# Two-mixer decoder layer: weight sums by adding DMAs, and x sums begun at the attention's end

## The chip, the cores and the metric

The kernel runs on one core of a Trainium2 chip. The metric is device microseconds of one execution, from outside the program; a profiled execution also gives the span from its first instruction to its last. A core has TensorE (PE, matmuls; its weight loads show as PEld), VectorE (DVE), ScalarE (ACT), GpSimd (POOL) and SyncE (SP), each with a queue of its own that is worked off in order, and 16 DMA engines.

## The reference, cut to what matters

One layer with two attention mixers, A (8 heads) and B (8 heads in 2 groups), on 512 tokens of width 1024, all float32:

```python
h = rms_norm(x, norm_w)
proj = h @ w_in                      # q, k, v, z of both mixers, ..., gate_m (2 * 1024 columns)
o_a = moba_mixer(...)                # block-sparse attention
o_b = nsa_mixer(...)                 # compressed, selected and window attention
y_a = o_a * silu(z_a);  y_b = o_b * silu(z_b)
g_m = sigmoid(gate_m)
merged = g_m[..., :1024] * (y_a @ w_branch_a) + g_m[..., 1024:] * (y_b @ w_branch_b)
x = x + merged @ w_out
```

The change concerns two of the products: the second half of `gate_m` (the gates of mixer B, `h` times a 1024x1024 part of `w_in`) and `merged @ w_out`.

## The kernel before, in words

Every large product is made with three fp32r matmuls (`mm3`, line 416): an operand is split in a high part `hi` and a rest `lo`, and hi·hi, hi·lo and lo·hi are summed in PSUM. A weight tile `wr` (128x512, 256 KB) is loaded by SP, ACT or POOL casts it to `wh` (lines 337 and 339), and DVE or POOL subtracts to get `wl` (line 341). The class `Stream` holds the list of all weight tiles in the order of their use, with 6 raw buffers and 8 pairs of `wh` and `wl`; a raw buffer becomes free for the next load when its `wl` is made.

The order of each engine's queue is fixed when the program is built. A planner in the kernel runs three generators (attention, projections and products, compression) against a clock `now`, in ns. A `Chain` is a row of steps; each step goes to the engine that the planner's costs say is done first, at the planner's time. So the planner's costs and times settle which engine does a step and where it stands. The hardware then waits for data, not for the planner's clock.

The stages, by the profile: the first projections, then the attention with projections as filler between its steps until about 338 us; the last gates of mixer A (`gmgate`); eight branch products of mixer A (`pbr`, 341 to 363 us), during which DVE also makes sums of x; the gates of mixer B (`gate_pair`, `pgw`) with the branch products of mixer B, to 425 us; and the output product (`last_wino`, `po`).

The steps of the attention that the prediction speaks of: for each unit (a head and a branch) DVE makes `sb` and row statistics, ACT makes `P` (exp), DVE the reciprocal `sst`, POOL multiplies `P` (line 992, four blocks of 512, 384, 256 and 128 columns; a small `p` where two units share a block), PE transposes it (`pt`, line 1001), ACT and DVE split the result in `ph` and `pl` (a last part is copied to `pf`), and PE multiplies with v into `O`.

The products with 1024x1024 weights are made by Winograd's form of Strassen's scheme: the weights are four quadrants a11, a12, a21, a22 and seven half-size products replace eight. It needs four sums of weight quadrants and four sums on the other side. Before, `Group` in the `Stream` makes the weight sums on the core: `ws` (line 378) from raw tiles in SBUF, by DVE or POOL, and `ws` is split like a raw tile. The x sums for mixer B's gates (`x_again`) start when both the attention and mixer A's gates are done: x is loaded again (`xa`), ACT scales it (line 1291), DVE and POOL make `ta` and `tb` (lines 1301 to 1305), and both are split into hi and lo (lines 1308 to 1313). `m_sums` does the same for the output product.

Lines that matter in the tail: 1392 (`gm` times `pbr`, which frees one of the two PSUM buffers of `pbr`), 1445 to 1449 (merge and split), 1481 to 1488 (`m_sums`) and 1519 (`xr`, the sum of a product into the output rows).

Of the kernel before, what the change touches and what calls it, by code (L numbers as in the profile page):

```python
# [18 lines left out]
S = 512  # L19
# [20 lines left out]
WGATES = True  # L40
WOUT = True
# [48 lines left out]
def hybrid_kernel(ctx: ExitStack, tc: tile.TileContext, x, x0, xT, wtok, wchan, gains, w1,  # L90
# [193 lines left out]
    class Group:  # L284


        def __init__(g, raws, outs):
            g.raws, g.outs = raws, outs
            g.uses = {}
            for o in outs:  # L290
                for z in (o,) if isinstance(o, int) else o[1:3]:
                    g.uses[z] = g.uses.get(z, 0) + 1

    class Stream:


        def __init__(w, entries, bufs, hi, lo):
            w.bufs, w.mk_hi, w.mk_lo = bufs, hi, lo
            w.raws, w.outs = [], []
            for e in entries:  # L300
                r0, o0 = len(w.raws), len(w.outs)
                if isinstance(e, Group):
                    w.raws += e.raws
                    w.outs += [(e, k, r0, o0) for k in range(len(e.outs))]
                else:
                    w.raws.append(e)
                    w.outs.append((None, 0, r0, o0))
            w.raw, w.out, w.chain, w.i, w.loaded, w.freed = {}, {}, {}, 0, 0, 0
            w.left, w.sums = {}, {}
# [9 lines left out]
        def used(w, r, when=None):  # L319
            if r in w.sums:  # L320
                w.sums[r][2] -= 1
                if not w.sums[r][2]:
                    release(w.sums[r][0], when)
                return
            w.left[r] -= 1
            if not w.left[r]:
                w.freed += 1
                while w.loaded < len(w.raws) and w.loaded - w.freed < w.bufs:
                    w.load()

        def halves(w, c, i, n, raw, src):
            hi, lo = w.mk_hi()[:, :n], w.mk_lo()[:, :n]
            w.out[i] = hi, lo

            def f(e):
                if e is nc.scalar:
                    e.copy(hi, raw())  # L337
                else:
                    e.tensor_scalar(hi, raw(), 1.0, 1.0, op0=ALU.mult, op1=ALU.mult)
            c.do({"A": ca(n), "P": 78 + n}, f).mark((w, 0, i))  # L340
            c.do(either(n), lambda e: e.tensor_sub(lo, raw(), hi.bitcast(F32))).mark((w, 1, i))  # L341
            c.call(lambda: w.used(src, c.t))

        def split(w, upto):
            while len(w.chain) < min(upto, len(w.outs)):
                i = len(w.chain)
                g, k, r0, o0 = w.outs[i]
                o = 0 if g is None else g.outs[k]
                n = w.raws[r0][1]
                rs = [r0 + z for z in ((o,) if isinstance(o, int) else o[1:3]) if isinstance(z, int)]  # L350
                while w.loaded <= max(rs, default=-1):
# [11 lines left out]
                st = w.sums[key] = [None, [], g.uses.get(me, 0) + 1, None]
                c = w.chain[i] = Chain(held=True)
                ready = [max(now[0], *(w.raw[r][1] for r in rs))]
                wait = [w.sums[o0, z] for z in (xa, xb) if not isinstance(z, int)]
                get = lambda z, r0=r0, o0=o0: (w.raw[r0 + z][0] if isinstance(z, int) else w.sums[o0, z][0])
                idx = lambda z, r0=r0, o0=o0: r0 + z if isinstance(z, int) else (o0, z)

                def go(c=c, ready=ready, wait=wait):  # L370
                    if all(z[3] is not None for z in wait):
                        c.start(max(now[0], *ready, *(z[3] for z in wait)))

                def f(e, st=st, op=op, a=get(xa) if isinstance(xa, int) else xa, b=get(xb) if isinstance(xb, int) else xb,
                      get=get, tag=tag, n=n):
                    a, b = (z if not isinstance(z, str) else get(z) for z in (a, b))
                    st[0] = alloc(tag, "ws")
                    (e.tensor_add if op == "+" else e.tensor_sub)(st[0][:, :n], a, b)  # L378

                def after(c=c, st=st, xa=xa, xb=xb, idx=idx):  # L380
                    st[3] = c.t
                    for z in (xa, xb):
                        w.used(idx(z), c.t)
                    for fn in st[1]:
                        fn()
                c.do(either(n), f, None, tag).call(after)
                w.halves(c, i, n, lambda st=st, n=n: st[0][:, :n], key)
                pend = [z for z in wait if z[3] is None]
                for z in pend:
                    z[1].append(go)  # L390
                if not pend:
                    go()
# [176 lines left out]
    for j in range(8):  # L569
        tiles += chan_tiles(f"gm{j}")  # L570
    tiles += [(wbr[j, 0], 512) for j in range(8)]
    for j in range(4):
        if WGATES:
            (a11, a12), (a21, a22) = (chan_tiles(f"gm{8 + j + i}") for i in (0, 4))
            tiles.append(Group([a11, a12, a21, a22, (wbr[j, 1], 512)], [
                0, 1, ("+", 2, 3, "s1", "sb"), ("-", "s1", 0, "s2", "sb"), ("-", 1, "s2", "s4", "sb"),
                ("-", 0, 2, "s3", "sb"), 4, 3]))
            tiles.append((wbr[j + 4, 1], 512))
        else:
            for i in (0, 4):  # L580
# [679 lines left out]

    gms = {}

    def gmgate(w, j):
        t = att("gm", F32)

        def emit(ps):
# [418 lines left out]
```

## Time and profile before

| | us |
|---|---|
| median of 3 runs (475.29 to 476.2) | 475.5 |
| the profiled execution, its own time | 475.35 |
| its span | 473.4 |

The time outside the span is 1.95 us. Busy times within the span:

| engine | busy us (share) | instructions |
|---|---|---|
| PE | 463.6 (98%) | 3172 |
| PEld | 424.5 (90%) | 3172 |
| DVE | 399.2 (84%) | 994 |
| ACT | 288.8 (61%) | 693 |
| POOL | 171.8 (36%) | 218 |

Matmuls overlap each other, so a time lost on PE is read from the starts of neighbouring matmuls, not from the busy share. In the rows below, the first column is the start in us from the span's start, the second how long the row lasted (of a row that merges several instructions, all together), and the bracket at the end tells how long the engine sat idle before it and who ended the wait. The granted TensorE clock was 1.00 throughout.

### The profile page before, as it was taken

To read this page: it belongs to the slowest core of one execution; us is meant where nothing else is said; L and a number is where in the kernel's file an instruction comes from. 1 tells how busy PE (TensorE), PEld (TensorE's weight loads), DVE (VectorE), ACT (ScalarE), POOL (GpSimd) and SP (SyncE) were. 2 spreads that over 40 slices of the span, in tenths; PEclk is the share of its full clock that TensorE was granted. 3 is DMA by queue.
4 is the path that set the end of the run, shared out by engine and by line. 5 is a ranking of instruction groups with operands and counts; after the bars stand their busy time and mean duration, and the time that the engine had idled before them with its cause. 6 is when DMAs were issued, how large, how long until landed. Compare 5 with 4: busy or idle time off the path is not lost.

```text
span 473.4 us, 9154 instructions
## 1 busy us (share of the span) xinstructions
PE 463.6 (98%) x3172; PEld 424.5 (90%) x3172; DVE 399.2 (84%) x994; ACT 288.8 (61%) x693; POOL 171.8 (36%) x218
## 2 busy tenths in 40 slices
PE   9999999999999999999999999999999999999897
PEld 9999898999999989888888888888887999999897
DVE  6888899798898579888787877778599799989994
ACT  8576694486876347576587457677483466444431
POOL 1254373048666105344446025464234023141000
PEclk9999999999999999999999999999999999999999
DMA  8916234444344423122212322201730442277551
GB/s 305 280 55 188 77 79 136 138 115 129 92 115 123 126 67 91 46 66 69 71 42 66 75 74 75 66 32 39 242 113 24 135 133 70 65 243 238 172 172 68
DMA packets 30206, 53.41 MB, mean 113 GB/s; under 512 B 3344, under 2 KB 5776, under 8 KB 30160
## 3 DMA queue, kind: packets, MB, share of 16 engines
q1 hardware_dynamic: 30160, 52.83, 37.1%
q8 instruction: 25, 0.41, 0.4%
q14 instruction: 21, 0.17, 0.1%
HBM read 50.06 MB, written 2.75 MB: 112 GB/s over the span
## 4 chain that ended last, share of the span: by engine, by line
PE 80%; DVE 13%; ACT 2%; issue 2%; POOL 2%; POOLq 0%; DVEq 0%
PE pgc L416 19%; PE pgt L416 18%; PE pgw L416 8%; PE O L1035 6%; PE pbr L416 6%; PE pt L1001 5%; DVE wl L341 4%; PE po L416 3%; PE sps L954 3%; PE sps L955 3%; PE pgf L631 3%; DVE ws L378 1%; DVE xr L1519 1%; PE pq L886 1%; PE pw L475 1%
## 5 line engine op out<-in xcount | busy, mean ns | idle before, releaser
L416 PE MATMUL pgt<-wh,hh 128*128 128x256 f32 (+1 forms) x288 | 82.9, 288 | 1.6 <-DVE X L772 0.9
L416 PE MATMUL pgt<-wl,hh 128*128 128x256 f32 (+1 forms) x288 | 81.4, 283 | 0.2 <-DVE wl L341 0.2
L416 PE MATMUL pgt<-wh,hl 128*128 128x256 f32 (+1 forms) x288 | 81.2, 282 | 0.0
L341 DVE TENSOR_TENSOR wl<-wr,wh 128x512 fp32r<-128x512 f32 (+1 forms) x108 | 75.3, 703 | 4.4 <-ACT wh L337 3.9
L992 POOL TENSOR_SCALAR P<-P,sst,gate 128x512 f32<-128x512 f32 (+3 forms) x56 | 39.6, 712 | 63.8 <-DVE sst L991 49.7
L973 DVE CUSTOM_DVE_ANT_0 sb<-sps,T 128x512 f32<-128x512 f32 (+3 forms) x96 | 46.1, 485 | 18.8 <-PE sps L955 17.8
L416 PE MATMUL pgc<-hh,wh 128*128 128x512 f32 x144 | 59.4, 413 | 0.0
L416 PE MATMUL pgc<-hl,wh 128*128 128x512 f32 x144 | 56.8, 395 | 0.0
L416 PE MATMUL pgc<-hh,wl 128*128 128x512 f32 x144 | 56.8, 395 | 0.0
L988 ACT ACTIVATE P<-sb,sst 128x512 f32<-128x512 f32 (+3 forms) x88 | 50.8, 578 | 9.6 <-DVE sst L973 9.0
L416 PEld LDWEIGHTS pgt<-wh,hh 128*128 128x128 f32 x288 | 54.2, 188 | 2.6 <-PE pgt L416 1.0
L416 PEld LDWEIGHTS pgt<-wh,hl 128*128 128x128 f32 x288 | 54.2, 188 | 0.5
L416 PEld LDWEIGHTS pgt<-wl,hh 128*128 128x128 f32 x288 | 54.2, 188 | 0.4 <-DVE wl L341 0.4
L1013 ACT CAST ph<-pt 128x512 fp32r<-128x512 f32 (+2 forms) x72 | 33.2, 479 | 34.9 <-PE pt L1001 34.1
L337 ACT CAST wh<-wr 128x512 fp32r<-128x512 f32 (+1 forms) x81 | 49.4, 616 | 0.4 <-DMA wr<-in_wtok 0.2
L992 POOL TENSOR_SCALAR P<-P,sst 128x512 f32<-128x512 f32 (+3 forms) x32 | 24.9, 782 | 44.3 <-DVE sst L991 37.8
L1001 PE MATMUL pt<-cst,P 128*128 128x128 f32 x232 | 40.7, 272 | 0.2 <-POOL P L992 0.2
L1015 DVE TENSOR_TENSOR pl<-pt,ph 128x512 fp32r<-128x512 f32 (+2 forms) x72 | 38.5, 550 | 2.2 <-ACT ph L1013 1.8
L458 POOL TENSOR_TENSOR nr<-nss,mhalf 128x4 f32<-128x4 f32 x28 | 29.5, 1057 | 24.6 <-DVE nss L457 24.2
L416 PE MATMUL po<-wl,mh 128*128 128x256 f32 x112 | 31.7, 283 | 1.9 <-DVE wl L341 1.9
L1001 PEld LDWEIGHTS pt<-cst,P 128*128 128x128 f32 x232 | 29.0, 140 | 4.5 <-POOL P L992 1.0
L416 PEld LDWEIGHTS pgc<-hl,wh 128*128 128x128 f32 x144 | 27.0, 188 | 6.4
(271 smaller groups left out, 1327.8 us busy)
## 6 DMA issues: line engine op xcount, KB each, us to landing
wr<-in_wchan SPq DMA_DIRECT2D x52, 256.0 KB, 2.6
wr<-in_wtok SPq DMA_DIRECT2D x36, 256.0 KB, 3.0
wr<-in_wout SPq DMA_DIRECT2D x24, 256.0 KB, 3.3
T<-rtab SPq DMA_DIRECT2D x16, 256.0 KB, 3.8
wr<-in_w SPq DMA_DIRECT2D x16, 256.0 KB, 2.7
wr<-in_wbr SPq DMA_DIRECT2D x16, 256.0 KB, 2.7
xr<-in_x SPq DMA_DIRECT2D x8, 256.0 KB, 4.9
out_y<-xr SPq DMA_DIRECT2D x16, 128.0 KB, 1.7
```

The lines of the kernel that those rows point to most:

```text
L337: e.copy(hi, raw())
L341: c.do(either(n), lambda e: e.tensor_sub(lo, raw(), hi.bitcast(F32))).mark((w, 1, i))
L416: nc.tensor.matmul(dst, sts[i][a], mvs[i][b], start=(start and i == a == b == 0), stop=(stop and i == n - 1 and b == 1), skip_group_check= ...
L458: c.do({"p": 430 + 150 * w}, lambda e: e.tensor_tensor(v(dst), v(ss), mhalf[:parts, :w], op=ALU.pow))
L631: nc.tensor.matmul(ps[t][:, :n], (hl if a else hh)[:, k, t * P:(t + 1) * P], ws[k][b], start=(k == a == b == 0), stop=(k == KT - 1 and b = ...
L973: e.tensor_tensor_reduce(z["sb"][:, :L], sps[:, :L], T[:, S - L:], scale=-1.0, scalar=3e38, op0=ALU.add, op1=ALU.min, accum_out=st[:, 0, b ...
L988: e.activation(pv(), z["sb"][:, :L], AF.Exp, bias=st[:, 0, b:b + 1], scale=-1.0, accum_out=st[:, 1, b:b + 1])
L992: c.do({"P": 315 + 0.834 * L}, lambda e: e.tensor_scalar(pv(), pv(), st[:, 2, b:b + 1], g, op0=ALU.mult, op1=ALU.mult))
L1001: nc.tensor.transpose(pt[:, (b - kb) * P:(b - kb + 1) * P], u.p0 if u.p0 is not None and b == 0 else u.pb[:, POFF[b] + kb * P:POFF[b] + (k ...
L1013: e.copy(z["w"][0], pt[:, :w])
L1015: ch.do({"D": cd(w)}, lambda e: e.tensor_sub(z["w"][1], pt[:, :w], z["w"][0].bitcast(F32)), pt)
L1035: nc.tensor.matmul(O[0][:, S - n:], v.bitcast(F32) if kb == 3 else v, w, start=(u.first and kb == 0 and i == 0), stop=(u.last and kb == 3 ...
```

## The change

- The four sums of weight quadrants are made in HBM, in two new DRAM tiles `wsum` (one for mixer B's gates, one for the output weights). For each of the eight sums ACT issues one DMA that copies a quadrant (1 MB) from HBM to HBM, and POOL issues two DMAs of half a quadrant each that add another quadrant, or another sum, to it (`accum_op=ALU.add`): 8 copies and 16 adding DMAs. All are put at times of the planner's clock, from 194 us on, a sum every 24 us.
- `Group` and the `ws` sums on DVE and POOL go. The `Stream` loads every operand of the seven products as a tile of its own: 9 loads instead of 6 for each of the four column blocks of the gates, 28 instead of 24 for the output weights, so SP issues 16 loads more.
- The sums are formed so that the weight side has only additions. The signs move to the other side: `x_sums` changes two orders of subtraction, `hi_lo` can negate (ACT with scale -1, DVE with a scalar-tensor-tensor for lo), and a tanh and an output sum take the minus sign.
- `x_again` is called when the attention ends, without waiting for mixer A's gates. The four pairs of x tiles start 6.5 us apart on the planner's clock, and only the sum that overwrites `hh` waits for mixer A's gates.
- Flags for versions without the scheme, and the code behind them, are removed.

```diff
+    wsum = [drp.tile([4, 4, P, 512], F32, name=nm("wsum")) for _ in range(2)]
+    def sum_weights():
+        flat = lambda z: z.rearrange("j p n -> (j p n)").rearrange("(r n) -> r n", n=2048)
+        jobs = []
+        for i in range(2):
+            (a11, a12, a21, a22), (s1, s2, s4, s3) = ([flat(z[k]) for k in range(4)] for z in (quads(i + 1), wsum[i]))
+            jobs.append((((s1, a21), (s3, a21), (s2, a11), (s4, a12)), ((s1, a22), (s3, a11), (s2, s1), (s4, s2))))
+        def copy(t, z):
+            Chain(t).call(lambda: nc.scalar.dma_start(out=z[0], in_=z[1], max_dma_last_dim=2048))
+
+        def add(t, z):
+            for r in range(2):
+                Chain(t + 8e3 * r).call(lambda r=r: nc.gpsimd.dma_start(
+                    out=z[0][r * 64:r * 64 + 64], in_=z[1][r * 64:r * 64 + 64], accum_op=ALU.add, max_dma_last_dim=2048))
+        for i in range(2):
+            for k in range(4):
+                copy(194e3 + 96e3 * i + 24e3 * k, jobs[i][0][k])
+                add(202e3 + 96e3 * i + 24e3 * k, jobs[i][1][k])
...
     for j in range(4):
-        if WGATES:
-            (a11, a12), (a21, a22) = (chan_tiles(f"gm{8 + j + i}") for i in (0, 4))
-            tiles.append(Group([a11, a12, a21, a22, (wbr[j, 1], 512)], [
-                0, 1, ("+", 2, 3, "s1", "sb"), ("-", "s1", 0, "s2", "sb"), ("-", 1, "s2", "s4", "sb"),
-                ("-", 0, 2, "s3", "sb"), 4, 3]))
-            tiles.append((wbr[j + 4, 1], 512))
...
+        for p_ in (1, 2, 5, 6, 3, 7):
+            tiles.append((operand(p_, 1, j), 512))
+        tiles += [(wbr[j, 1], 512), (operand(4, 1, j), 512), (wbr[j + 4, 1], 512)]
+    for p_, c in [(p_, c) for p_ in (1, 2) for c in range(2)] + [(p_, c) for c in range(2) for p_ in (5, 6, 3, 7, 4)]:
+        tiles += [(operand(p_, 2, 2 * c + i), 512) for i in range(2)]
...
+    def hi_lo(c, z, hi, lo, neg):
+        n = z.shape[-1]
+        if neg:
+            c.do({"A": 93 + ca(n)}, lambda e: e.activation(hi, z, AF.Copy, scale=-1.0))
+            c.do({"d": cd(n)}, lambda e: e.scalar_tensor_tensor(lo, z, -1.0, hi.bitcast(F32), op0=ALU.mult, op1=ALU.subtract))
...
     def x_again():
-        if not WGATES or "att" not in done or "gma" not in done:
-            return
...
-            c2.call(lambda c=c, c1=c1, c2=c2: c.start(max(c1.t, c2.t)))
+            T1[k] = Chain(held=True)
+            hi_lo(T1[k], ta[:, h[0]], hh[:, k, h[1]], hl[:, k, h[1]], 0)
+            TX[1, k] = hh[:, k, h[1]], hl[:, k, h[1]], T1[k]
+            c2.call(lambda c=c, c1=c1, c2=c2, t=now[0] + 6.5e3 * k: c.start(max(c1.t, c2.t, t)))
```

PE's queue holds the same instructions on the same operands in the same order before and after. On POOL and ACT the queues up to the attention's end are the old ones with the DMAs put in. The first place is POOL's queue at the third and fourth adding DMA (lines 992 and 931 are the multiplication of `P` before and after, 339 and 316 the cast of a weight tile). Before:

```order
L992 TENSOR_SCALAR P_3579<-P_3579,sst_3553,gate 128x512
L992 TENSOR_SCALAR P_3579<-P_3579,sst_3553,gate 128x384
L339 TENSOR_SCALAR wh_3666<-wr_3335 128x512
L992 TENSOR_SCALAR P_3579<-P_3579,sst_3553,gate 128x256
L992 TENSOR_SCALAR P_3678<-P_3678,sst_3682,gate 128x512
L992 TENSOR_SCALAR P_3678<-P_3678,sst_3682,gate 128x384
L992 TENSOR_SCALAR P_3678<-P_3678,sst_3682,gate 128x256
L992 TENSOR_SCALAR p_3755<-p_3755,sst_3739,gate 128x128
L992 TENSOR_SCALAR P_3678<-P_3678,sst_3682,gate 128x128
```

The same place of POOL's queue in the changed kernel (`in_wgate` holds the quadrants of the gates' weights):

```order
L931 TENSOR_SCALAR P_3585<-P_3585,sst_3559,gate 128x512
L523 DMA wsum_158<-in_wgate 256x512
L931 TENSOR_SCALAR P_3585<-P_3585,sst_3559,gate 128x384
L316 TENSOR_SCALAR wh_3673<-wr_3339 128x512
L931 TENSOR_SCALAR P_3585<-P_3585,sst_3559,gate 128x256
L931 TENSOR_SCALAR P_3685<-P_3685,sst_3689,gate 128x512
L931 TENSOR_SCALAR P_3685<-P_3685,sst_3689,gate 128x384
L523 DMA wsum_158<-in_wgate 256x512
L931 TENSOR_SCALAR P_3685<-P_3685,sst_3689,gate 128x256
L931 TENSOR_SCALAR p_3763<-p_3763,sst_3746,gate 128x128
L931 TENSOR_SCALAR P_3685<-P_3685,sst_3689,gate 128x128
```

The third adding DMA now stands ahead of the 384 block of one unit, and the fourth ahead of the 256 block of the next; nothing else moved here.

The second place is DVE's queue during the last branch products of mixer A, around its sixth product with a gate (line 1392 before, 1347 after). Before:

```order
L1392 SCALAR_TENSOR_TENSOR gm_4529<-gm_4529,pbr_5249 128x512
L1304 TENSOR_TENSOR tb_5129<-xa_5126,xa_5124 128x256
L1309 TENSOR_TENSOR T_5098<-ta_5121,T_5098 128x256
L1309 TENSOR_TENSOR hl<-ta_5128,hh 128x256
L1313 TENSOR_TENSOR th_5123<-tb_5122,T_5097 128x512
L1392 SCALAR_TENSOR_TENSOR gm_4713<-gm_4713,pbr_5278 128x512
L1305 TENSOR_TENSOR tb_5129<-xa_5126,ta_5128 128x256
L1309 TENSOR_TENSOR th_5130<-ta_5128,th_5130 128x256
L378 TENSOR_TENSOR ws_5330<-wr_5210,wr_5254 128x512
```

After:

```order
L1347 SCALAR_TENSOR_TENSOR gm_4544<-gm_4544,pbr_5270 128x512
L318 TENSOR_TENSOR wl_5293<-wr_5213,wh_5292 128x512
L1229 TENSOR_TENSOR hl<-ta_5117,hh 128x256
L1226 SCALAR_TENSOR_TENSOR T_5094<-ta_5117,T_5094 128x256
L1218 TENSOR_TENSOR tb_5118<-ta_5117,xa_5115 128x256
L1214 TENSOR_TENSOR ta_5124<-xa_5120 128x256
L1347 SCALAR_TENSOR_TENSOR gm_4729<-gm_4729,pbr_5294 128x512
L1215 TENSOR_TENSOR ta_5124<-xa_5122,ta_5124 128x256
L1229 TENSOR_TENSOR th_5119<-tb_5118,T_5093 128x512
```

The sums of the last x pair, most of which stood ahead of the sixth product, now stand behind it, and the weight sum `ws` is gone.

The third place is DVE's queue in the output product, from the split of the last sums of `merged` on (line 1488 before, 1229 after; lines 1519 and 1465 are the sum into the output rows). Before:

```order
L1488 TENSOR_TENSOR ml_6185<-mb_6181,mh_6184 128x512
L378 TENSOR_TENSOR ws_6342<-wr_6280,wr_6255 128x512
L1519 SCALAR_TENSOR_TENSOR xr_6147<-po_6327,xr_6147 128x256
L378 TENSOR_TENSOR ws_6354<-wr_6300,ws_6332 128x512
L341 TENSOR_TENSOR wl_6283<-ws_6332,wh_6282 128x512
L1519 SCALAR_TENSOR_TENSOR xr_6147<-po_6348,xr_6147 128x256
L378 TENSOR_TENSOR ws_6377<-wr_6323,ws_6342 128x512
L341 TENSOR_TENSOR wl_6285<-ws_6342,wh_6284 128x512
```

After:

```order
L1229 TENSOR_TENSOR ml_6210<-mb_6206,mh_6209 128x512
L318 TENSOR_TENSOR wl_6352<-wr_6287,wh_6351 128x512
L318 TENSOR_TENSOR wl_6354<-wr_6316,wh_6353 128x512
L1465 SCALAR_TENSOR_TENSOR xr_6173<-po_6355,xr_6173 128x256
L1465 SCALAR_TENSOR_TENSOR xr_6173<-po_6377,xr_6173 128x256
L318 TENSOR_TENSOR wl_6395<-wr_6324,wh_6394 128x512
L318 TENSOR_TENSOR wl_6397<-wr_6361,wh_6396 128x512
```

The `ws` rows between the splits are gone, and each `wl` is made from a loaded tile `wr`.

More of the change, by code (lines that the diff above doesn't have):

```diff
@@ L281, in all_of, with __init__ @@
         return f
[L284 to L292, printed above, removed]
-    class Stream:
[L297 to L307, printed above, removed]
+    class Stream:
+        def __init__(w, raws, bufs, hi, lo):
+            w.raws, w.bufs, w.mk_hi, w.mk_lo = raws, bufs, hi, lo
             w.raw, w.out, w.chain, w.i, w.loaded, w.freed = {}, {}, {}, 0, 0, 0
-            w.left, w.sums = {}, {}
         def load(w, force=False):
@@ L317, in load, with used @@
                 w.loaded += 1
[L319 to L323, printed above, removed]
-                return
[L325 to L342, printed above, removed]
+        def used(w):
+            w.freed += 1
+            while w.loaded < len(w.raws) and w.loaded - w.freed < w.bufs:
+                w.load()
@@ L344, in split @@
         def split(w, upto):
-            while len(w.chain) < min(upto, len(w.outs)):
+            while len(w.chain) < min(upto, len(w.raws)):
                 i = len(w.chain)
[L347 to L351, printed above, removed]
+                if w.loaded <= i:
@@ L363, in split @@
[L363 to L392, printed above, removed]
+                raw, t = w.raw[i]
+                n = w.raws[i][1]
+                hi, lo = w.mk_hi()[:, :n], w.mk_lo()[:, :n]
+                w.out[i] = hi, lo
+                c = w.chain[i] = Chain(max(now[0], t))
@@ L394, in take, with f @@
+                def f(e, hi=hi, raw=raw):
+                    if e is nc.scalar:
+                        e.copy(hi, raw)
+                    else:
+                        e.tensor_scalar(hi, raw, 1.0, 1.0, op0=ALU.mult, op1=ALU.mult)
+                c.do({"A": ca(n), "P": 78 + n}, f).mark((w, 0, i))
+                c.do(either(n), lambda e, hi=hi, lo=lo, raw=raw: e.tensor_sub(lo, raw, hi.bitcast(F32))).mark((w, 1, i))
+                c.call(w.used)
         def take(w, n, width):
@@ L1261, in hybrid_kernel, with gmgate @@
     gms = {}
-    def gmgate(w, j):
+    def gmgate(j):
         t = att("gm", F32)
@@ L1275, in xrows, with t1_try @@
         return xT[(k - 1) * P:k * P, :] if k else x0[:, :S]
+    def t1_try(k):
+        if "gma" in done and ("ta", k) in done:
+            T1[k].start(max(done["gma"], done["ta", k]))
     def x_again():
-        if not WGATES or "att" not in done or "gma" not in done:
-            return
         T3 = [alloc("T", "T3", dt=F32R) for _ in range(2)]
-        TXheld.extend(T3)
-        pools = [alloc("ph", "T1", dt=F32R) for _ in range(3)] + [sp.tile([P, S], F32R, name=nm("T2"), tag="pl", bufs=3) for _ in range(3)]
-        TXheld.extend(pools[:3])
+        pools = T3 + [alloc("ph", "T1", dt=F32R) for _ in range(3)]
+        TXheld.extend(pools)
+        pools = pools + [sp.tile([P, S], F32R, name=nm("T2"), tag="pl", bufs=3) for _ in range(3)]
+        h = (slice(0, 256), slice(256, 512))
         for k in range(4):
@@ L1434, in gemms @@
         for j in range(8):
-            yield from gmgate(0, j)
+            yield from gmgate(j)
         done["gma"] = now[0]
-        x_again()
+        for k in range(4):
+            t1_try(k)
         for j in range(8):
@@ L1468, in gemms @@
             yield from merge(j + 4)
-        yield from (last_wino if WOUT else last)(ms, xr)
+        yield from last(ms, xr)
     mt = {}
```

160 lines of the change are left out of this document (50 added, 110 removed).

## The prediction

> **What bounds the kernel now.** I read the page first, then the waits of PE by stage, then PE's timeline at the waits, last the queues of the engines that PE waited for.
>
> ```profile
> span 473.4 us, 9154 instructions
> ...
> PE 463.6 (98%) x3172; PEld 424.5 (90%) x3172; DVE 399.2 (84%) x994; ACT 288.8 (61%) x693; POOL 171.8 (36%) x218
> ```
>
> PE is busy nearly all the time, so only a moment in which PE waits can be won, and each new wait on PE is lost. From 195 to 341 us, the stretch into which the new DMAs are put, the list of PE's waits has one entry of note:
>
> ```profile
> PEld pt L1001 <- POOL P L992: 0.6, 1, 0.6
> ```
>
> So the attention has nothing to give back, and its one wait is for POOL, the queue that gets the adding DMAs. After 341 us the list is longer, all on DVE:
>
> ```profile
> PE po L416 <- DVE wl L341: 1.9, 2, 1.3
> PE pbr L416 <- DVE gm L1392: 0.8, 1, 0.8
> PE po L416 <- DVE ml L1449: 0.7, 1, 0.7
> PE po L416 <- DVE xr L1519: 0.2, 1, 0.2
> ```
>
> The timeline gives the exact loss: a 512-column matmul starts 0.23 us after its neighbour, a 256-column one 0.12.
>
> ```profile
> 360.19 0.40 PE L416 MATMUL pbr<-yl,wh 128*128 128x512 f32 x1
> 361.38 0.47 PE L416 MATMUL pbr<-yh,wh 128*128 128x512 f32 x1 [0.79 <-DVE gm L1392]
> ...
> 427.43 0.39 PE L416 MATMUL po<-wh,mh 128*128 128x256 f32 x1
> 428.54 0.39 PE L416 MATMUL po<-wh,ml 128*128 128x256 f32 x1 [0.73 <-DVE ml L1449]
> ...
> 438.93 0.28 PE L416 MATMUL po<-wh,ml 128*128 128x256 f32 x1
> 440.50 0.39 PE L416 MATMUL po<-wl,mh 128*128 128x256 f32 x1 [1.29 <-DVE wl L341]
> ...
> 441.20 0.28 PE L416 MATMUL po<-wh,ml 128*128 128x256 f32 x1
> 442.04 0.39 PE L416 MATMUL po<-wl,mh 128*128 128x256 f32 x1 [0.56 <-DVE wl L341]
> ```
>
> Start to start, less a normal step: 1.19 - 0.23 = 0.96, 1.11 - 0.12 = 0.99, 1.57 - 0.12 = 1.45, 0.84 - 0.12 = 0.72, and 0.2 for `xr`: 4.3 us in all, the most that the end can give (about 0.5 more if the slow first matmul after each wait, 0.39 instead of 0.28, goes too).
>
> **The change part by part.** *The weight sums leave DVE.* In the output product, DVE's groups from 424 us on hold 16 of them:
>
> ```profile
> L1519 DVE SCALAR_TENSOR_TENSOR xr<-po,xr 128x256 f32<-128x256 f32 x28 | 11.4, 413 | 3.5 <-PE po L416 3.5
> ...
> L378 DVE TENSOR_TENSOR ws<-wr,ws 128x512 f32<-128x512 f32 x8 | 5.4, 677 | 0.0
> L378 DVE TENSOR_TENSOR ws<-wr,wr 128x512 f32<-128x512 f32 x8 | 5.3, 677 | 0.0
> ```
>
> That is 10.7 us less work on the engine that PE waits for there. The `wl` of the fifth and sixth product no longer stand behind `ws`, so 1.45 + 0.72 go, and the 0.2 at `xr`. At 427 us PE waits for the split of `merged`, ahead of all `ws`; there one 0.6 us row of DVE (line 1488) leaves the way, so I take 0.6 of 0.99. The 15 `ws` in the gates (up to 424 us) pay nothing, since PE has no wait there. What is late next at the end is nothing that I can see.
>
> *The x sums.* The wait at 361.38 is for DVE's sixth `gm`, which stood behind the sums of all four x pairs. In the new order 14 rows of 512 columns and 18 of 256 stand between the last gate `gm` of `gmgate` and this row; by the durations above that is 14 x 0.68 + 18 x 0.41 = 16.9 us from 341, so the row can run at 358, and the buffer was wanted at 360.4. The 0.96 goes. The four pairs' tail is covered by two products (24 matmuls of 0.12) before the first sum of x is used.
>
> *The adding DMAs on POOL.* POOL's profile of before has no DMA, so I bound the time that issuing one keeps POOL from its next instruction. From below: SP's issue of a weight tile. From above: POOL's own long rows, which are long while DVE works. Between: POOL's two-operand row.
>
> ```profile
> L227 SPq DMA_DIRECT2D wr<-in_wchan x52: 327/328/981, 18.4 to 400.9; - x52
> ...
> L341 POOL TENSOR_TENSOR wl<-wr,wh x8: 1283/1302/3306, 61.7 to 407.2; 128x512 fp32r<-128x512 f32 x8
> ```
>
> So 0.33 to 3.31 us; I take 1.3, the median of the last row, since it is the row of POOL's own queue with two inputs, as an addition has, and most POOL rows aren't stretched. What 1.3 costs depends on the place. Of the twelve in the attention, four have less than 2 us of slack up to PE's transposes:
>
> ```profile
> 230.65 0.77 POOL L992 TENSOR_SCALAR P<-P,sst,gate 128x512 f32<-128x512 f32 x1 [2.18 <-DVE sst L991]
> 232.85 0.66 POOL L992 TENSOR_SCALAR P<-P,sst,gate 128x384 f32<-128x384 f32 x1 [1.43 <-DVE sst L991]
> ...
> 238.89 1.95 POOL L992 TENSOR_SCALAR P<-P,sst,gate 128x512 f32<-128x512 f32 x3 [3.21 <-DVE sst L991]
> 240.97 0.45 POOL L992 TENSOR_SCALAR p<-p,sst,gate 128x128 f32<-128x128 f32 x1
> 241.39 0.45 POOL L992 TENSOR_SCALAR P<-P,sst,gate 128x128 f32<-128x128 f32 x1
> ...
> 289.58 1.30 POOL L1076 TENSOR_TENSOR yl<-ys,yh 128x512 fp32r<-128x512 f32 x1 [0.56 <-ACT yh L1075]
> 290.86 1.20 POOL L992 TENSOR_SCALAR P<-P,sst,gate 128x384 f32<-128x384 f32 x2
> ...
> 330.05 1.73 POOL L992 TENSOR_SCALAR P<-P,sst,gate 128x384 f32<-128x384 f32 x2 [0.98 <-DVE sst L991]
> ```
>
> ```profile
> 235.74 0.55 PE L1001 MATMUL pt<-cst,P 128*128 128x128 f32 x3 [0.24 <-POOL P L992]
> ...
> 242.37 0.60 PE L1001 MATMUL pt<-cst,P 128*128 128x128 f32 x4
> ...
> 292.99 0.27 PE L1001 MATMUL pt<-cst,p 128*128 128x128 f32 x1
> ...
> 332.65 0.27 PE L1001 MATMUL pt<-cst,p 128*128 128x128 f32 x1
> ```
>
> The third DMA comes at 231.42 with 1.43 us of idle time behind it and PE waiting already: slack 1.43. The fourth comes inside the merged row of 238.89, ahead of its last block: 0.13 idle before `p`, and 242.37 - 241.84 = 0.53 to PE, 0.66 in all. The eighth: 0.56 idle, then 292.99 - 292.06 = 0.93, so 1.49. The eleventh, ahead of a cast: 0.98, then 332.65 - 331.78 = 0.87, so 1.85. The other eight stand ahead of idle times of 2 us and more, or ahead of casts used much later, and cost nothing up to 3 us. PE has no other idle time here to win a delay back, so with an issue of D us the loss is the sum of what D exceeds these four slacks by: for 1.3 it is 0.64, for 2 it is 0.57 + 1.34 + 0.51 + 0.15 = 2.6, for 3.31 it is 1.88 + 2.65 + 1.82 + 1.46 = 7.8.
>
> The Trainium skill speaks on both sides. "DMA: Bandwidth & Descriptors", section "Anatomy of one DMA", calls descriptor generation on GpSimd "small, variable" and puts most of a DMA's 2 us into the write receipt; by it, with D at the low end and no slack passed, the sum would be 471.5. "SBUF — State Buffer", in "SBUF: two separate sides", says that GpSimd can't write descriptors while DVE holds the port they share, and tells of 0.62 us grown to 3.1; by it, as an estimate, the sum would be 475.35 - 3.9 + 7.0 = 478.5. The POOL rows of 1.28 and 3.31 us for one form agree with the second in kind, though no DMA stands among them.
>
> An adding DMA also waits for its copy, and what is queued behind it on POOL, the `P` blocks and casts, waits with it. The third DMA's copy is issued by ACT behind a tanh that ends at 223.8, 7.6 us ahead. ACT's row, and the nearest landings (KB each, median us from issue to landing):
>
> ```profile
> 223.13 0.63 ACT L1253 ACTIVATE th<-zs 128x512 f32<-128x512 f32 x1
> ```
>
> ```profile
> wr<-in_wchan SPq DMA_DIRECT2D x52, 256.0 KB, 2.6
> ...
> wr<-in_wout SPq DMA_DIRECT2D x24, 256.0 KB, 3.3
> ...
> xa<-in_xT SPq DMA_DIRECT2D x7, 256.0 KB, 5.9
> ```
>
> A 1 MB copy moves 2 MB, like the eight x tiles issued back to back, so I take 5.9: no wait. Up to 7.6 us it costs nothing. SP's 16 added loads and the longer landing beside the copies are hidden by five tiles of lookahead, each 12 matmuls of 0.12 or 1.4 us, 7 us against a landing of 2.6 to 5.9; without that cover each tile would cost PE 1 us or more.
>
> *The copies on ACT.* By SP's row 0.33 to 0.98 us of ACT each. Only the third stands ahead of a step that PE needs soon:
>
> ```profile
> 248.06 0.25 ACT L893 COPY pf<-pt 128x128 f32<-128x128 f32 x1
> ...
> 248.59 0.38 PE L1035 MATMUL O<-pf,vb 128*128 128x128 f32 x2
> ```
>
> Slack 248.59 - 248.31 = 0.28, so 0.05 (0.7 at the upper end); I take the median, 0.33. The other five stand ahead of steps with time to spare, or behind idle time of ACT.
>
> *After 341 us on POOL.* The last four adding DMAs stand ahead of casts and of the `wl` of the eighth branch product. The first of them waits for a copy that ACT issues behind five scalings of x and a cast:
>
> ```profile
> 343.34 1.95 ACT L1291 ACTIVATE xa<-xa,wcol 128x512 f32<-128x512 f32 x3
> ```
>
> Six rows of 0.6 from 343.3 give 347, and 5.9 for the landing 353; with 1.3 for the issue and 3.3 for the slowest `wl` POOL is done at 357.6, and PE starts that product at 361.4. The cover is 3.8 us; without it PE would wait by as much as the copy is later. The last two wait for a copy issued during the first gates, ahead of casts that PE uses a column block later, some 10 us: nothing.
>
> *What else moves.* The eight loads of x stand one branch weight earlier in SP's queue, so that one 256 KB load comes behind them: it is the weight of a branch product that starts 15 us later, no cost. Negated splits keep their sizes; ACT and DVE have the time, since the row that limited them, `ws`, is gone. Casts that move to POOL in the output product take POOL's free time, as the row of that stretch shows (its fields are PE, PEld, DVE, ACT and POOL, each with busy us and instructions):
>
> ```profile
> 424.00:473.40 49.40, 43.46 (x347) 41.90 (x345) 43.14 (x87) 16.86 (x29) 2.55 (x2) 1.00 0.52 167
> ```
>
> POOL was busy for 2.55 of 49.4 us.
>
> **The sum.** Against the profiled execution's 475.35 (the median of the runs is 475.5): - (0.96 + 0.60 + 1.45 + 0.72 + 0.2) = -3.9, + 0.64 + 0.05 = +0.7, so 472.1.
>
> **The rivals.** *Slower: POOL's issue is stretched beside DVE.* D = 3.31 gives 475.35 - 3.9 + 7.85 = 479.3. It decides from D = 2.3 on (all four slacks passed: 4 x 2.3 - 5.43 = 3.8, the gain). For it speaks the 3306 in POOL's row, against it that the median there is 1302. *The end finds a new wait.* The output product loads 28 tiles where it loaded 24, beside output rows; if PE then waits for a DMA instead of for `ws`, only 0.96 + 0.6 are won: 475.35 - 1.6 + 0.7 = 474.5. Against it: a tile of 256 KB lands in about 2.6 to 3.4 us and five are under way. *Late copies.* If 1 MB lands after 11 us instead of 5.9, the third adding DMA waits 3.4 us on POOL, and 3.3 us pass to PE (with the issue, 4.7 less 1.43): 475.4, no change.
>
> **How the numbers follow.** Forecast 0.55 (its own range 470.5, all waits gone and cheap issue, to 474, D = 1.95); stretched issue 0.23; new wait at the end 0.11; late copies 0.11. A measurement of this kernel tells about 0.2%, 0.95 us, from no change, so faster is below 474.4 and slower above 476.3 (from D = 2.6). Faster: nearly all of the first case and half of the new waits, 0.60. Slower: most of the stretched issue and a little of the late copies, 0.23. Same: 0.17. The range for 8 in 10 runs from 470.5 to the stretched issue's 479.3.
>
> **What would show it.** Right: no `ws` rows, PE's waits after 341 us down from 3.6 to under 1 us, `po` no longer waiting for `wl`; at most one new wait of `pt` for POOL near 242, and POOL's DMAs near 1.3 us. Wrong: many waits of `pt` on POOL in the attention, POOL waiting for a DMA ahead of an adding DMA, or `po` and `pgw` waiting for casts of late tiles.

## The result and the profile after

The changed kernel takes 472.98 us (median; 471.18 to 475.0), the kernel before on the same chip 475.64: ratio 0.9938, 95% interval 0.9919 to 0.9957, so 0.6% faster, and clear of no change. 472.1 was forecast, with 470.5 to 479.3 as the range. The profiled execution took 473.72, so it is 0.7 above its median; its span and its busy times:

```profile
span 471.9 us, 9247 instructions
...
PE 463.5 (98%) x3172; PEld 424.2 (90%) x3172; DVE 386.5 (82%) x972; ACT 281.1 (60%) x683; POOL 184.5 (39%) x242
```

DVE lost 12.7 us of work, POOL has 12.7 us more. PE's waits after 341 us were four entries with 3.6 us in all. Now the list has one:

```profile
PE pbr L343 <- ACT hh L1228: 1.4, 1, 1.4
```

So po waits for nothing any more, but pbr waits longer than before. The timeline of PE shows it, and one new wait in the attention:

```profile
243.00 0.40 PE L343 MATMUL pgc<-hl,wh 128*128 128x512 f32 x1
243.46 0.66 PE L940 MATMUL pt<-cst,P 128*128 128x128 f32 x4
...
361.31 0.40 PE L343 MATMUL pbr<-yl,wh 128*128 128x512 f32 x1
363.06 0.47 PE L343 MATMUL pbr<-yh,wh 128*128 128x512 f32 x1 [1.35 <-ACT hh L1228]
```

Start to start, less 0.23: 0.23 us at 243, 1.52 us at 361 (0.96 before). The bracket names ACT's hh, the last to end by the profile (362.99), but this matmul doesn't read hh. It needs the PSUM buffer that DVE's gm of 362.24 frees, and it starts 0.15 us behind that row's end (362.91), as in the kernel before (361.38 behind 361.23). The timeline of DVE shows why this gm is late:

```profile
356.35 0.67 DVE L1347 SCALAR_TENSOR_TENSOR gm<-gm,pbr 128x512 f32<-128x512 f32 x1
356.95 0.68 DVE L318 TENSOR_TENSOR wl<-wr,wh 128x512 fp32r<-128x512 f32 x1
357.55 1.52 DVE L1229 TENSOR_TENSOR hl<-ta,hh 128x256 fp32r<-128x256 f32 x1
358.99 1.55 DVE L1226 SCALAR_TENSOR_TENSOR T<-ta,T 128x256 fp32r<-128x256 f32 x1
360.47 1.51 DVE L1218 TENSOR_TENSOR tb<-ta,xa 128x256 f32<-128x256 f32 x1
361.90 0.41 DVE L1214 TENSOR_TENSOR ta<-xa 128x256 f32<-128x256 f32 x1
362.24 0.68 DVE L1347 SCALAR_TENSOR_TENSOR gm<-gm,pbr 128x512 f32<-128x512 f32 x1
```

Three rows of 256 columns, 0.41 each elsewhere, take 1.5: 3.3 us lost in a row ahead of gm. POOL's timeline at that place:

```profile
357.00 1.79 POOL L318 TENSOR_TENSOR wl<-wr,wh 128x512 fp32r<-128x512 f32 x1 [3.93 <-ACT wh L314]
358.73 0.87 POOL L523 DMA_DIRECT2D wsum<-wsum  x1
359.35 0.91 POOL L316 TENSOR_SCALAR wh<-wr 128x512 fp32r<-128x512 f32 x1
360.35 1.35 POOL L318 TENSOR_TENSOR wl<-wr,wh 128x512 fp32r<-128x512 f32 x1
```

Each slow row of DVE ends some 0.28 us behind a row of POOL (359.07 behind 358.79, 360.54 behind 360.26, 361.98 behind 361.70): DVE stood still until POOL's row was done. This is called the lock below. The Trainium skill, "SBUF — State Buffer", section "SBUF: two separate sides", calls the port that the two share an exclusive lock, held for a whole instruction, and names DVE's rows with two SBUF inputs against POOL's that read SBUF. These rows agree, and so do the `gm` rows of the branch products, with one input from PSUM: 0.67 to 0.69 in every profile here, also beside rows of POOL.

Where the 1.8 us of the trace come from, by the start of the same matmul in the timelines (PE's queue is the same in all kernels; us later than in the profiled run of before, negative is earlier; the columns are times in the kernel before):

```
                163.0  357.6  361.4  391.5  418.1  460.3
changed          0.77   1.16   1.68   1.80   1.83  -1.80
e5_control       0.36   1.35   0.33   1.84   1.86  -1.88
e1_no_sums       0.05   0.04  -0.95  -1.09  -1.07  -4.95
e4_no_last       0.25   0.56  -0.43  -0.59  -0.59  -4.23
e7_early        -0.15  -0.15  -1.15  -1.31  -1.30  -4.98
```

The output product (418 to 460) wins 3.63. (The span is only 1.4 us shorter: from PE's last matmul to the end it takes 3.5 us here and 3.1 before.) The first 0.77 are lost ahead of 163 us, where all five queues are those of before: that differs from run to run (-0.17 to 1.18 over the kernels here), and part of it is why this run lies above its median.

The adding DMAs, by line (duration ns min/median/max, first and last start), and DMA issues (KB each, median us to landing):

```profile
L523 POOL DMA_DIRECT2D wsum<-wsum x8: 873/892/1233, 255.9 to 379.5; - x8
...
L523 POOL DMA_DIRECT2D wsum<-in_wgate x4: 855/886/1139, 206.1 to 241.1; - x4
L523 POOL DMA_DIRECT2D wsum<-in_wout x4: 853/880/907, 305.8 to 334.8; - x4
```

```profile
wsum<-in_wgate ACTq DMA_DIRECT2D x4, 1024.0 KB, 5.5
wsum<-wsum POOLq DMA_DIRECT2D x8, 512.0 KB, 6.5
wsum<-in_wout ACTq DMA_DIRECT2D x4, 1024.0 KB, 6.3
```

### The profile page after: what moved, and what is told of

It reads as the page before. It is cut to its first block, busy times and chain, and to the rows that moved or that the text cites. A ratio compares the mean times of both kernels' runs of the same rounds, so it can differ in the third digit from the quotient of the medians.

```text
span 471.9 us, 9247 instructions
## 1 busy us (share of the span) xinstructions
PE 463.5 (98%) x3172; PEld 424.2 (90%) x3172; DVE 386.5 (82%) x972; ACT 281.1 (60%) x683; POOL 184.5 (39%) x242
## 4 chain that ended last, share of the span: by engine, by line
PE 80%; DVE 8%; ACT 5%; POOL 2%; DMA 2%; issue 1%; SPq 0%; POOLq 0%; DVEq 0%; ACTq 0%
PE pgc L343 18%; PE pgt L343 17%; PE pgw L343 9%; PE po L343 8%; PE pbr L343 7%; PE O L974 6%; PE pt L940 5%; PE sps L893 3%; PE sps L894 3%; DVE wl L318 2%; PE pq L825 1%; POOL P L931 1%; DMA wr<-in_w 1%; DMA x<-in_xT 1%; ACT wh L314 1%
## 5 line engine op out<-in xcount | busy, mean ns | idle before, releaser
L318 DVE TENSOR_TENSOR wl<-wr,wh 128x512 fp32r<-128x512 f32 (+1 forms) x139 | 97.3, 714 | 6.5 <-ACT wh L314 5.1
L314 ACT CAST wh<-wr 128x512 fp32r<-128x512 f32 (+1 forms) x98 | 59.1, 615 | 17.2 <-DMA wr<-wsum 11.7
L316 POOL TENSOR_SCALAR wh<-wr 128x512 fp32r<-128x512 f32 (+1 forms) x50 | 39.4, 795 | 76.1 <-DMA wr<-wsum 31.0
```

Source lines behind the costliest of these rows:

```text
L314: e.copy(hi, raw)
L316: e.tensor_scalar(hi, raw, 1.0, 1.0, op0=ALU.mult, op1=ALU.mult)
L318: c.do(either(n), lambda e, hi=hi, lo=lo, raw=raw: e.tensor_sub(lo, raw, hi.bitcast(F32))).mark((w, 1, i))
```

## The experiments

All are edits of the changed kernel and have its queue of PE. Ratios are to the kernel before, run on the same chip.

**What do the sums cost, and where?** Four kernels, run together.

e1_no_sums:

```diff
-    ... 5: lambda: s_[0, j], 6: lambda: s_[1, j], 3: lambda: s_[2, j], 7: lambda: s_[3, j] ...
+    ... 5: lambda: quads(w)[2, j], 6: lambda: quads(w)[3, j], 3: lambda: quads(w)[1, j], 7: lambda: quads(w)[0, j] ...
...
-    sum_weights()
```

> All 8 copies and 16 adding DMAs are left out; in place of each sum a single quadrant is loaded, so the products are not those of the reference. PE's queue and DVE's are as in the changed kernel. Theory: the DMAs cost PE 0.3 us at 243 us (the P blocks behind the fourth adding DMA) and part of the 1.5 us at 361 us, because POOL's rows, held up to 350 us by the wait for a copy, then run beside DVE's and hold these up; so 471.2 to 472.6 against the 473.0 of the changed kernel, with the wait at 361 below 0.5. Rival 1, the wait at 361 is a matter of DVE's order alone: 472.6, and it stays at 1.2 to 1.5. Rival 2, the traffic of the sums slows weight loads all over: below 471.

Measured 470.86 us (ratio 0.9886, 0.9868 to 0.9904). From 195 us on PE's list of waits has only the 0.2 us at 236 that was there before. All of the forecast gain and more is there (4.95 in the trace), and the DMAs cost the changed kernel some 2 us of it; 470.86 lies a little below the theory's range, not because of loads all over (by the table PE is at 0.04 at 357.6 us, so the attention gained nothing) but because the wait at 361 goes whole.

e2_quarters:

```diff
             for r in range(2):
-                Chain(t + 8e3 * r).call(lambda r=r: nc.gpsimd.dma_start(... 64 rows, accum_op=ALU.add ...))
+                for u in range(2):
+                    q_ = r * 64 + u * 32
+                    Chain(t + 8e3 * r).call(lambda q_=q_: nc.gpsimd.dma_start(... 32 rows ...))
```

> Each adding DMA of 512 KB is issued as two of 256 KB, at the same place of POOL's queue; nothing else moves. The changed kernel's adding DMAs last 0.89 us each, but the next POOL row starts 0.64 us after the DMA's start. Theory, a fixed price per DMA and the slacks of the prediction (1.43, 0.66, 1.49, 1.85): two in a row hold the next row for 1.3 to 1.55 us, so the loss at the fourth place grows from 0.3 to 0.65 to 0.9 and the others stay near zero: 473.3 to 473.7. Rival 1, the price goes with the bytes: 473.0, rows of 0.45 us. Rival 2, the issue is stretched beside DVE when there are more of them: single rows over 2 us and a total of 475 or more.

Measured 474.62 us (0.9965, 0.9951 to 0.9979), 1.6 more than the changed kernel and above the theory's 473.7. PE at the fourth and the eighth place:

```profile
243.33 0.66 PE L942 MATMUL pt<-cst,P 128*128 128x128 f32 x4 [0.93 <-POOL P L933]
...
294.77 0.55 PE L942 MATMUL pt<-cst,P 128*128 128x128 f32 x3 [0.47 <-POOL P L933]
```

Two of half the size take 1.67 us, one of the whole size 0.88: the price is per DMA, and the rival by bytes falls. The slack rule holds at the fourth place with the DMA's whole row as its price: 0.88 - 0.66 = 0.22 for the 0.23 of the changed kernel, 1.67 - 0.66 = 1.01 for the 1.09 here. (The 0.64 from the DMA's start to the next row's start was too low a price: that row then lasts longer, until the DMA is done.) The loss of 0.40 at 236, there in the kernel before, is gone in this run. The eighth was to stay near zero, gives 1.67 - 1.49 = 0.18 by the rule, and loses 0.64. POOL there:

```profile
290.01 1.67 POOL L525 DMA_DIRECT2D wsum<-wsum  x2
291.15 1.86 POOL L1017 TENSOR_TENSOR yl<-ys,yh 128x512 fp32r<-128x512 f32 x1
292.45 2.27 POOL L933 TENSOR_SCALAR P<-P,sst,gate 128x384 f32<-128x384 f32 x2
```

The subtraction yl ends at 293.01, 1.3 behind the DMAs' end: that is its usual time. The two blocks of P then need 1.71 us more, until 294.72, where they need 1.16 in the changed kernel: 0.55 more, which the rule doesn't count. That the moved rows meet other rows of DVE is likely, but not shown. After 341 us this run loses 0.47 near 355 and 1.24 near 387 and nothing at 361, in sum about what the changed kernel loses there.

e3_x_late:

```diff
     def x_again():
+        if "att" not in done or "gma" not in done:
+            return
...
-            c2.call(lambda ..., t=now[0] + 6.5e3 * k: c.start(max(c1.t, c2.t, t)))
+            c2.call(lambda ..., t=now[0]: c.start(max(c1.t, c2.t, t)))
```

> The sums of x begin again when both the attention and mixer A's gates are done, all four pairs at once, as in the kernel before; the weight sums stay with the DMAs. Theory: the early start wins nothing, since DVE is busy without a break from 345 to 366 us either way and PE's wait at 361 us comes from rows of DVE that POOL holds up; the time stays within 0.6 us of 473.0, with a wait of 0.5 to 2 us near 361. Rival, the prediction's own step (the early start takes 0.96 us away): 474 or more, with a wait near 361 that is about 1 us longer than the changed kernel's.

Measured 472.74 us (0.9931, 0.9913 to 0.9948), no difference. The wait at 361 is gone; one of 1.12 stands a product earlier (at the matmul that starts at 357.59 in the kernel before), and one of 0.53 at 391. With the late sums of weights in place, the early start of the x sums wins nothing. Whether it does without them is e11.

e4_no_last:

```diff
-            for k in range(4):
+            for k in range(4 if i == 0 else 2):
                 copy(...); add(...)
...
+        if w == 2 and p_ in (6, 3):
+            return quads(2)[2 if p_ == 6 else 1, j]
```

> The last two sums of the output weights are left out (2 copies, 4 adding DMAs, all after 341 us); a quadrant is loaded in place of each, so those products are not the reference's. DVE's queue is as in the changed kernel. Theory: POOL no longer waits until 350 us for a copy, its two-operand rows run earlier, and the three rows of DVE that took 1.5 us each from 357.5 on take 0.4: the wait at 361 falls from 1.5 to below 0.5, and the time to 471.8. Rival: POOL's rows hold up DVE in any case, the adding DMAs have no part in it: the wait stays at 1 us or more, 473.0.

Measured 470.24 us (0.9877, 0.9860 to 0.9895). The wait at 361 is gone, as the theory has it, and the time is below its 471.8. POOL's wait to 350 us was not the reason, though: its subtraction starts at 350.30 here too, since it waits for its cast. Of the 16 adding DMAs, the last four carry nearly the whole price.

**Is it the place?** Four more, run together.

e5_control is the changed kernel, nothing edited.

> The changed kernel once more, unchanged. Theory: whether POOL's subtraction near 357 us gets ahead of DVE's rows isn't settled by the queues, so the wait at 361 us may come out anywhere from 0 to 1.7 us (it was 1.5), while the wait of 0.2 us at 243 and the short tail (3.6 us less than before from 424 us on) come again; 472 to 474. Rival: the order settles it, and the wait is 1.4 to 1.6 us again.

Measured 473.08 us (0.9934, 0.9914 to 0.9955). The same program with the same queues loses its time elsewhere: 0.23 at 243, 0.50 at 355, no wait at 361, and 1.57 us at 391. The list of PE's waits after 341 us:

```profile
PE pgw L344 <- DVE gm L1321: 1.4, 1, 1.4
PE pbr L344 <- DVE gm L1348: 0.3, 1, 0.3
```

In this profile POOL's subtraction waits until DVE's rows are done (3.13 us), and a row of DVE at 350.80, held for 2.2 us, stands ahead of the 0.50 at 355. So the order doesn't settle the wait at 361. The one at 391 begins with a late weight tile, by the timelines of SP and ACT:

```profile
381.50 1.22 SPq L224 DMA_DIRECT2D wr<-in_wgate  x2
```

```profile
389.84 0.62 ACT L315 CAST wh<-wr 128x512 fp32r<-128x512 f32 x1 [3.34 <-DMA wr<-in_wgate]
```

The load took 8 us, beside two adding DMAs issued at 379.1 and 380.3. The stretch from 378 to 392 us by windows (DMA share is the second field from the end) and the loads issued in it with their median us to landing, in e5_control and then in e7_early:

```profile
378.00:392.00 14.00, 13.37 (x93) 12.13 (x92) 11.19 (x24) 7.32 (x16) 2.44 (x3) 1.00 0.91 224
```

```profile
wr<-in_wgate SPq DMA_DIRECT2D x2, 256.0 KB, 8.7
```

```profile
378.00:392.00 14.00, 14.00 (x103) 13.25 (x102) 12.84 (x26) 7.57 (x16) 3.01 (x2) 1.00 0.46 149
```

```profile
wr<-in_wgate SPq DMA_DIRECT2D x3, 256.0 KB, 2.6
```

e6_ws_back:

```diff
+                if i in dummy:      # the 16 tiles of sums of the output weights
+                    ... e.tensor_tensor(ws, raw, raw, op=ALU.max), then hi and lo from ws
```

> The 16 sums of the output weights stay with the DMAs, but each loaded sum is passed once more through DVE (the maximum of the tile with itself into a buffer ws, 0.68 us, ahead of its split): the work that the change took from DVE is put back, with the same result. Theory, the prediction's second step: the waits of PE for wl and ml after 424 us come back, 2.8 to 3.7 us, so 475.8 to 476.7. Rival, the tail gained because the splits no longer wait for two loads of one sum: the waits stay away, 473.0.

Measured 476.33 us (1.0004, 0.9989 to 1.0019), 3.25 more than the control of the same call. PE's waits from 424 us on:

```profile
PE po L353 <- DVE wl L328: 1.4, 2, 0.8
PE po L353 <- ACT wh L324: 0.4, 1, 0.4
```

The gain of the output product is DVE's freed time: put that work back, and by the medians it is gone. The profiled run is the fastest of the twelve (474.70); its output product still keeps 1.0 of the 3.63.

e7_early:

```diff
-                copy(194e3 + 96e3 * i + 24e3 * k, jobs[i][0][k])
-                add(202e3 + 96e3 * i + 24e3 * k, jobs[i][1][k])
+TIMES = ((170.5e3, 194e3, 196e3), (184.5e3, 209.5e3, 213.5e3), (195e3, 220e3, 224.7e3), (216.5e3, 238e3, 244e3),
+         (230.5e3, 258e3, 258.2e3), (244.4e3, 267e3, 267.2e3), (259.3e3, 275.6e3, 287e3), (273.8e3, 300e3, 307.5e3))
+        for n_, (t, t0, t1) in enumerate(TIMES): copy(t, ...); add((t0, t1), ...)
```

> The same 8 copies and 16 adding DMAs at times of their own: each adding DMA ahead of a row of POOL that waited at least 1.5 us for other work in the run without sums, the copies ahead of waits of ACT, all issued before some 313 us; DVE's and PE's queues are the changed kernel's. Theory: the price of the sums is only where they stand, so nearly all of what the run without sums won comes: 470.5 to 471.3, no wait of PE at 243 and none over 0.3 at 361. Rival, the traffic or the issues cost something wherever they stand: 472 or more. Rival for 361, luck of the port: a wait of 1 to 1.6 us there, and 472.

Measured 470.65 us (0.9880, 0.9865 to 0.9896): 2.4 us faster than the changed kernel on the same chip, with the same sums, and level with the kernel without any sums. It is the best version here that computes the layer. POOL and DVE where the lock was:

```profile
355.69 3.12 POOL L320 TENSOR_TENSOR wl<-wr,wh 128x512 fp32r<-128x512 f32 x1 [3.93 <-ACT wh L316]
```

```profile
357.63 0.69 DVE L1348 SCALAR_TENSOR_TENSOR gm<-gm,pbr 128x512 f32<-128x512 f32 x1
```

Here it is POOL that stands still (3.12 instead of 1.28), and the gm that PE waits for runs at 357.63.

e8_no_pool:

```diff
+                if 345e3 < c.t < 362e3 and len(cost) > 1:
+                    cost = {k: n for k, n in cost.items() if k != "P"}
```

> For steps of the planner between 345 and 362 us POOL isn't chosen: its three subtractions, a sum of x and a cast near 350 to 361 us go to DVE and ACT; the adding DMAs stay. DVE gets some 2.2 us more to do there. Theory, DVE's rows were held up by POOL's: no row of DVE over 0.8 us from 345 to 363 but beside an adding DMA, and the wait at 361 under 0.6 although DVE has more to do: 471.8 to 472.5. Rival, DVE simply has too much to do there: the wait grows to 2 us or more, 473.5 or more.

Measured 472.59 us (0.9920, 0.9905 to 0.9934). No wait at 361, no row of DVE over 0.75 us from 347 to 364, with more work on DVE: "too much to do" falls, and with the rows above the lock is what made the wait. (The control's profile, of the same call, has no wait at 361 either, so without the rows this run would not settle it.) The wait at 391 is left (0.54), and the time is 0.1 above the theory's range.

**What of the last four adding DMAs is it?** Three run together, and one more.

e9_tiny and e10_traffic (both with e4's replacement of the two sums):

```diff
 e9_tiny
+                late = i == 1 and k > 1
+                copy(..., (z0[:2], z1[:2]) if late else (z0, z1))
+                add(..., 1 if late else 64)          # rows of 8 KB
 e10_traffic
+                if i == 1 and k > 1:
+                    for r in range(2):
+                        copy(202e3 + 96e3 * i + 24e3 * k + 8e3 * r, (spare, quadrant))
+                else: add(...)
```

> The last two sums of the output weights keep all their instructions at their places in every queue, but the two copies move 16 KB and the four adding DMAs 8 KB each; quadrants are loaded in place of the two sums, so those products are not the reference's. Theory T, the traffic: after 341 us the DMA engines were busy 0.84 to 0.91 of the time in the changed kernel, and x and weight tiles come late; without the bytes the time falls to 470.2 to 470.9 as in the run without the last sums, and no wait over 0.3 us is left at 361 and 391. Theory P, POOL's issue of the four DMAs beside DVE: the time stays at 472.3 to 473.2, with a wait near 361 or 391 us.

> The last two sums keep their copies; in place of each of the four adding DMAs ACT issues a plain copy of a quadrant (1 MB, to a buffer that nobody reads), so the bytes on the way are at least as many and POOL issues nothing after 341 us; quadrants are loaded in place of the two sums. Theory T, the traffic: 472 to 473.5, with a wait of 0.5 us or more near 361 or 391. Theory P, POOL's issue: 470.2 to 471, no such wait.

Measured 471.38 us for e9 (0.9901, 0.9877 to 0.9925), with no wait at 361 or 391 but 0.80 at 448 in its profile (a late tile of the output product, and xr behind it), and 470.94 for e10 (0.9891, 0.9867 to 0.9915), with no wait after 341 us, though the DMA share was 0.92 from 341 to 352 us and 0.79 from 378 to 392. So neither the four instructions alone (e9) nor the bytes alone (e10) bring the waits: each theory has one run against it. In e9 the time is still 0.5 above theory T's range, by the wait at 448.

e11_early_x_late is e7 with e3's edit.

> The sums of weights at their early places (the kernel of 470.65), and the sums of x begun as in the kernel before, when mixer A's gates are done. Theory, the prediction's step for the sums of x holds where nothing else disturbs: the wait at 361 is back with 0.5 to 1.2 us, 471.1 to 471.9. Rival: the early start of the sums of x wins nothing by itself, the weight sums taken from DVE did it: 470.4 to 470.9, no wait.

Measured 472.98 us (0.9929, 0.9906 to 0.9951), above the ranges of both theories. Its one wait of pbr:

```profile
PE pbr L345 <- DVE gm L1349: 1.0, 1, 1.0
```

1.12 us start to start, but not at 361: PE starts again at 358.80, with the matmul of 357.59 in the kernel before, and waits for the fifth `gm`; the place at 361, where the sixth is waited for, loses nothing. So a late start of the x sums does cost a wait when the weight sums are out of the way, and in the profile of e7, with the early start, there is none. It isn't the 0.96 that the prediction meant, and POOL has its part in it: two rows of DVE ahead of that `gm` last 0.93 and 1.51 instead of 0.41, 1.6 us in all. The rest of the 2.3 us to e7 is mostly a wait of 1.15 at 449 us in the output product; that this belongs to the edit isn't shown.

e12_adds_only (with e4's replacement):

```diff
+                if i == 1 and k > 1:
+                    add(202e3 + 96e3 * i + 24e3 * k, (s3, quadrant))    # no copy ahead of it
```

> The last two sums' copies are left out, their four adding DMAs stay at their places with their full 512 KB each, but add a quadrant to the sum s3, which is long done, so that none waits for a late copy; the products with s2, s4 and s3 are not the reference's. What is open: the four DMAs with 8 KB each cost little (471.4), plain copies of the same bytes cost nothing (470.9), the change as it stands 473.0. Theory A, a full-size adding DMA by itself (its descriptors and its two reads and a write beside late loads): 472 to 473.2, a wait over 0.4 us near 361 or 391. Theory B, POOL's wait for a late copy, which puts the DMAs and the rows behind them late: 470.3 to 471.3, no such wait.

Measured 472.13 us (0.9912, 0.9893 to 0.9931), two of its six runs at 470.9, four at 472.1 to 472.8. Its profiled run repeats the changed kernel's wait at 361 to the last digit (1.52), with DVE's three rows at 1.52, 1.55, 1.52 and POOL's ahead of them:

```profile
356.38 1.78 POOL L318 TENSOR_TENSOR wl<-wr,wh 128x512 fp32r<-128x512 f32 x1 [3.94 <-ACT wh L314]
358.11 0.87 POOL L525 DMA_DIRECT2D wsum<-in_wout  x1
```

So the wait comes without a late copy too, and the two groups of runs fit a lock that comes or doesn't. That the adding DMA brings it isn't shown. With the x sums in the changed order, four profiles have a full-size adding DMA behind this subtraction: in two of them (the changed kernel and this one) POOL got in ahead of DVE's three rows (1.79 and 1.78), in two (e5 and e6) it did not (3.13 and 3.12). In the six without such a DMA (e1, e2, e4, e7, e9, e10) it never did (3.12 to 3.14). But the subtraction starts ahead of that DMA in all of them. No wait at 391 here. Open stays what settles who gets the port first, and which of copies and adding DMAs makes the loads at 380 late.

## Why the prediction was nearly right

- *Weight sums off DVE.* Right, too small: 0.60 + 1.45 + 0.72 + 0.2 = 2.97 forecast, 3.63 in the trace, 3.25 by the medians when put back (e6). The wait for ml went whole, 0.99 and not 0.60, and the slow restarts went with the waits.
- *The x sums' 0.96.* This is the step that failed: the wait became 1.52. Its estimate (gm can run at 358) holds to 0.4 us where POOL's subtraction waits for DVE (357.63 in e7). But the estimate added DVE's rows at their own durations, while POOL's rows beside them held DVE for 3.3 us more. The row of before that should have warned stands in the prediction: POOL's wl of 1283/1302/3306 ns. I read 3306 as POOL's loss only; the lock works both ways, and DVE pays when POOL is first. The prediction also had the old wait's cause by half: it named only what stood ahead of the sixth `gm`. DVE, then POOL, in the kernel before:

```profile
357.35 0.92 DVE L1304 TENSOR_TENSOR tb<-xa,xa 128x256 f32<-128x256 f32 x1
358.19 1.51 DVE L1309 TENSOR_TENSOR T<-ta,T 128x256 fp32r<-128x256 f32 x1
```

```profile
354.67 3.31 POOL L341 TENSOR_TENSOR wl<-wr,wh 128x512 fp32r<-128x512 f32 x1 [5.76 <-issue]
358.13 1.29 POOL L341 TENSOR_TENSOR wl<-wr,wh 128x512 fp32r<-128x512 f32 x1 [0.15 <-ACT wh L337]
```

The two rows of DVE end some 0.28 us behind POOL's and lost 1.6 us, more than the 0.96 that PE waited. At their usual 0.41 the `gm` would, by these rows, have ended at 359.6, ahead of the 360.4 at which PE wanted the buffer. The same holds for each wait of pbr in these profiles: rows of DVE held by POOL stand ahead of it, for 1.6 us in e3 and e11, 2.2 in e5 and e2, 3.3 in the changed kernel and e12.
- *"After 341 us on POOL": cover 3.8, cost nothing.* The cover held (the copy was in by 349.9, earlier than 353), but it was the wrong question. Without the last two sums the time is 2.7 us lower (e4), with all sums ahead of idle rows 2.4 (e7 against e5); they cost it by DVE's rows in one run and by a load of 8 us in another. The lookahead that was to hide loads of 2.6 to 5.9 us broke there.
- *POOL's issue.* D = 1.3 forecast; 0.89 measured (0.85 to 1.23). Only the fourth place lost time, 0.23 instead of 0.64, as the rule gives it for 0.89. The stretch beside DVE did not come (3.31 was its bound). The Trainium skill's page "SBUF — State Buffer", section "Who interferes with whom", limits that stretch to DVE's two-port modes and infers that a two-input row leaves descriptor writing alone; 16 issues with none over 1.23 us, and 32 of half the size with the longest at 1.75, agree.
- *Copies.* Landing 5.9 forecast, 5.5 and 6.3 measured; no wait at the third place. ACT's issue is 0.50, not 0.33, and cost nothing.
- *The sum.* From -3.2: -0.66 (end), -0.41 (issue), -0.05 (ACT), +1.52 (361: 0.96 not won, 0.56 lost), +0.3 of small ones make -2.5, the 0.77 from ahead of 163 us left aside; the medians differ by 2.66. Errors of both signs cancelled, so 0.9 us of distance flatters the working.

## What to carry to other kernels

Give DMAs of a busy engine a place by that engine's idle rows in a trace, not by even times: here the same 24 DMAs cost 2.4 us at even times and, ahead of idle rows, nothing that these runs can tell (470.65 against 470.86 without sums). Where VectorE is the engine that others wait for, count GpSimd's rows beside VectorE's rows with two SBUF inputs as VectorE's own time, and when you clear a wait of 1 us by reordering, ask what else runs on the other side of the shared port at that moment. Run the same kernel twice before explaining one wait: the same queues put the loss at 361 us in one run and at 391 in the next.

## What the hardware showed

- An adding DMA from HBM to HBM takes its issuer 0.85 to 1.23 us with 512 KB, 0.79 to 1.75 with 256 KB (two back to back 1.67 together) and 0.77 at the least with 8 KB, and by the page's list of queues (packets, MB, share of 16 engines; q0 holds the adding DMAs, q10 the copies) it takes the DMA engines twice as long per byte:

```profile
q0 software_dynamic: 4352, 8.39, 10.9%
q10 hardware_dynamic: 4224, 8.39, 5.3%
```

- Six plain copies of 1 MB issued after 341 us, at a DMA share of 0.62 to 0.92 beside the weight loads, cost PE nothing (e10): from 378 to 392 us loads of weight sums landed in 5.8 us (median) instead of 2.8 in e7, and PE didn't wait.
- 0.41 us rows of VectorE took 1.5 us three times in a row, each ending 0.28 us behind a row of GpSimd, while the `gm` rows with one input in PSUM took 0.67 to 0.69 in every profile.
